# One hybrid decoder layer: gate ranks transposed a tile ahead, level copies ahead of the last doubling, one scaling moved to ScalarE

## The chip, the core and the metric

The kernel runs on one core of a Trainium2 chip. The metric is the device time in microseconds (us), the median over runs. The engines are named as in the profile: PE is TensorE (PEld its weight loads), DVE is VectorE, ACT is ScalarE, POOL is GpSimd, SP is SyncE, whose queue issues the DMA transfers. Each engine works through its own list of instructions in order; what another engine has to deliver is waited for by semaphores.

## The reference

One layer of a decoder with two groups of heads side by side, for 2048 prompt tokens and 64 sample tokens (8 sequences of 8), width 1024. Group A is attention in a window of 128 with a learned sink per head (8 query heads, 2 key heads, 64 wide), group B is gated linear attention (GLA, 4 heads, keys 64 wide, values 128 wide) whose gate has rank 16. An output projection and a squared-ReLU MLP (4096 wide) follow.

```python
# group A, softmax with a sink
m = jnp.maximum(jnp.max(scores, axis=-1, keepdims=True), sink)
p = jnp.exp(scores - m)
p = p / (jnp.sum(p, axis=-1, keepdims=True) + jnp.exp(sink - m))
# group B, log gate from the ranks, and the recurrence over chunks
log_a = jax.nn.log_sigmoid(jnp.einsum('btr,rk->btk', glr, w_gk2) + b_gk) / GLA_GATE_TEMP
S = ab[..., None] * S + jnp.einsum('bthk,bthv->bhkv', kd, vv)
o = rms_norm(o, g_gla) * jax.nn.silu(gr)
mix = jnp.einsum('bte,ed->btd', jnp.concatenate([attn, gla_out], axis=-1), w_out)
```

All matmuls are to float32's precision; the kernel splits operands into a high and a low part (fp32r), which is what names such as `ph`, `pl`, `wop` and `mt` stand for.

## The kernel before

The prompt is worked in tiles of 128 tokens (16 of them, `NB`), the sample tokens are one more tile. There are four stages, one behind the other.

**Attention (about 40 to 300 us).** The loop over tiles `i` holds four units per tile, one for each pair of query heads, (r, jj) = (0,0), (0,1), (1,0), (1,1), u = 0 to 3. The generator `unit` is one unit, cut into phases by its `yield`s: scores `sc` (PE), the mask and the maximum (DVE, into `s` and `m`), exp with the sum `den` (ACT), reciprocal and the scaling of `s` by `den` (DVE, two instructions of 128x256), transposes `pT` of `s` (PE), the copy `ph` (ACT) and the rest `pl` (DVE), the products `av` (PE), and the sum `mo` (ACT copy `rest`, then DVE). Units overlap: for each u the loop steps the units `now`, `behind` and `ahead` by their phases and puts between them the input projection's matmuls (`proj`, as many as `A_FILL` says) and other work of the tile (`A_PLAN`). The order so written holds on PE, ACT and DVE: `te`, `ac` and `dv` are `InOrder` wrappers that tie each instruction to the one before it. One step of the loop, at u, is: `next(now)`, `next(behind, None)`, `next(ahead)`, `next(now)`; the `ahead` step there is the next unit's `sc`, and the second `next(now)` is this unit's `pT`.

**GLA (about 345 to 740 us).** The generator `gla(i)` works one tile and hands back counts of filling matmuls; the main loop puts so many matmuls of the GLA projection (`gproj`) there. `G_FILL` holds the five counts. Here the order of PE follows the program, while ACT's and DVE's instructions are placed by a scheduler, within what the program's dependencies and `tc.issue_after` ties allow. What a tile does, in order:

- `qk_T`: transposes of queries and keys (`gqk`), copies `kt` (DVE) and `qz` (ACT). 34 fills follow.
- `finish_out` of the tile before: squares `ojunk` (ACT), root, `og` (DVE), transposes `ogT` (PE), copy `mo` (ACT), store.
- `decays(i + 1)` for the next tile: in even tiles of two the ranks are transposed (`pg`, PE) and copied (`glrT`, ACT), one copy for two tiles. 6 fills follow. Then the two products `z` (PE), three activations `zt` (ACT) and `before` (DVE). The second fill count stands between `pg` and `z`.
- `put_diagonal` (DVE, into AH) and the levels: for each of seven block sizes `level_sums` doubles the running sums. Per level there are two exps (ACT, `dec`, from `before` L1011 and `after` L1013) and two additions (DVE, `after` L1014 and `before` L1015), and `weighted` (DVE, `XK`, `XQ`). In the program they belong to this tile; the scheduler lets the next tile's doublings run while this tile's fills run. With the last level, `keys_decayed` makes `kdT` (ACT exp L997, DVE product) and later transposes it (PE) and copies it to `kd` (ACT L1003).
- `gate` (`sg`: ACT, DVE and two products on POOL). Then 24 fills, the `kdT` transposes, 8 fills.
- level products `gl` and `gh` (PE), the state's increment `ds` (PE, from `kd`), `qd` (DVE), the six `put_level` writes into AH (DVE, predicated copies L1021), two far copies and two near copies into AT (all ACT, L1122 and L1124; a near copy moves one half, 64x256), the two updates of the state S (DVE, L1127). 20 fills.
- `o`: four pairs of matmuls per tile, from S and `qd`, and from AT.

From tile 6 on, parts of the output weight are also split (`wop`, one 128x1024 ACT copy and one DVE subtraction each; `WO_PARTS`), tied behind `done`, the last S update. The raw part `wor` is loaded and the result `wo_d` stored by SP's queue.

PSUM is shared by `bank(shape, kind)`: a tile of a kind waits until the last one of the kind in its slot has been read. `decays(i, P, before)` uses kind "d", as do `gqk` and `ds`; `keys_decayed`, `o` and `ogT` use "e".

**Output projection and MLP (from about 740 us).** PE works them through nearly without a gap; the change leaves this code as it is.

Lines that the text below refers to: `G_FILL` L65, the scaling in `unit` L489, the loop's step L835 to L838, `decays` L933, `keys_decayed` L995, `level_sums` L1011 to L1015, `put_level` L1021, `decayed` L1060, `gla` L1067, AT L1122 and L1124, S L1127.

Of the kernel before, what the change touches and what calls it, by code (L numbers as in the profile page):

```python
# [15 lines left out]
AF = mybir.ActivationFunctionType  # L16
ALU = mybir.AluOpType
# [4 lines left out]
P = 128  # L22
# [3 lines left out]
NB = T // P  # L26
# [15 lines left out]
NL = len(LEVELS)  # L42
# [19 lines left out]
G_FIRST = (0, 1)  # L62
G_NEXT = (NB, *range(2, NB))
G_ORDER = (0, 1, 2, 3)
G_FILL = (34, 6, 24, 8, 20)  # L65
S_WAIT = (3, 6)
WO_PARTS = ((), (0, 1, 2), (3, 4, 5), (6, 7))
B_ORDER = (*(j + b for j in range(4) for b in (0, 4)), NB, *(j + b for j in range(4) for b in (8, 12)))
# [47 lines left out]
def f32(ap):  # L116
    return ap.bitcast(F32)
# [23 lines left out]
def hybrid_step_kernel(ctx: ExitStack, tc: tile.TileContext, I, O):  # L141
    nc = tc.nc
# [20 lines left out]
    te, ac, dv = (InOrder(tc, engine) for engine in (nc.tensor, nc.scalar, nc.vector))  # L163
# [4 lines left out]
    def bank(shape, kind, name):  # L168

        return ps.tile(shape, F32, tag=kind, name=name, bufs=1 if kind in "de" else 2)  # L170
# [21 lines left out]
    ident = cpool.tile([P, P], F32, name="ident")  # L192
# [77 lines left out]
    glr = gp_pool.tile([P, (NTILE + 1) // 2, 2, HD], F32R, name="glr")  # L270
# [185 lines left out]
    def unit(i, r, jj, mo):  # L456
# [29 lines left out]
        yield  # L486
        dv.reciprocal(den, den)
        for u in range(2):
            dv.tensor_scalar(s[:, u, :nk], s[:, u, :nk], den[:, u : u + 1], None, op0=ALU.mult)  # L489
        yield  # L490
        pT = bank([P, nkt, 2, P], "c", f"pT_{u_}")
        for u in range(2):
# [289 lines left out]
    for i in range(NB):  # L782
        if i + 4 < NTILE:
            load_x(i + 4)
        if i == NB - 1:
            wa_pool.release()
            w_pools.append(open_gw(G_LATE))
            for n in range(4):
                stage = ("w_raw", 2) if n % 2 else ("x", 2)
                weights.append((*load_gw(*late.popleft(), *stage), stage))  # L790
        elif i >= 3:
            for _ in range(min(2, len(early))):
                weights.append((*load_gw(*early.popleft()), None))
        store()
        if i == 4:
            wgk, msk, smsk, dmsk, onehot, ggla = load_consts()
        if i == NB - 4:
            nc.sync.dma_start(smask, I["c_smask"])
            cached.update({(name, 0): load_cache(name, 0) for name in "kv"})
        if i >= NB - 2:  # L800
            t = i - NB + 2
            gxTs[t] = load_T(t, [sp.tile([P, KT, P], F32R, tag=x, name=f"g{x}_{t}", bufs=2) for x in ("xh", "xl")])
            fill = chain(fill, projecting(t, gxTs[t], G_EARLY, ac))
        new = i + 3 < NTILE
        todo["turn"] = lambda: run(rotate(i + 1))
        if i + 2 < NTILE:
            todo["first"] = lambda: take_first(i + 2)
            todo["rest"] = lambda: todo.update(vl=take_rest(i + 2))
        if new:
            todo["junk"] = lambda: todo.update(rstd=x_norm(i + 3))  # L810

        def do(u, phase):
            for name, at in A_PLAN:
                if at == (u, phase) and name in todo:
                    todo.pop(name)()

        for u in range(4):
            for unit_ in (behind, now) if u in A_PL_FIRST else (now, behind):
                next(unit_, None)
            next(now)  # L820
            do(u, "A")
            later = next(queue)
            next(later)
            run(fill, A_FILL[u][0])
            next(behind, None)
            next(behind, None)
            run(fill, A_FILL[u][1])
            if u < 2 and new:
                hi, todo[f"x{u}"] = x_half(i + 3, u)
                hi()  # L830
            elif u == 2:
                todo.update(heads_T(i + 1))
            do(u, "X")
            run(fill, A_FILL[u][2])
            next(now)  # L835
            next(behind, None)
            next(ahead)
            next(now)  # L838
            do(u, "B")
            split_some(A_SPLIT[u] if i < NB - 1 else 1)  # L840
            next(now)
            do(u, "C")
            behind, now, ahead = now, ahead, later
# [86 lines left out]
    for t in (s_xk, s_qz, s_at, s_after):  # L930
        nc.gpsimd.memset(t, 0.0)

    def decays(i, n, before, kind="d"):  # L933

        gt = glrT[i // 2 % 2 if i < NB else 2]
        if i % 2 == 0:
            pg = bank([P, P], kind, f"pg_{i}")
            te.transpose(pg, f32(glr[:, i // 2]).rearrange("p a r -> p (a r)"), ident)
            nc.scalar.activation(gt, pg, AF.Copy)
        yield  # L940
        z = bank([P, 2, n], kind, f"z_{i}")
        for g in range(2):
            te.matmul(z[:, g], wgk[:, i % 2, g * P : (g + 1) * P], gt[:, :n], start=True, stop=True)
        t = next(zts)[:, :, :n]
        nc.scalar.activation(t, z, AF.Abs)
        nc.scalar.activation(t, t, AF.Exp, scale=-1.0)
        nc.scalar.activation(t, t, AF.Ln, bias=1.0)
        nc.vector.scalar_tensor_tensor(before, z, 0.0, t, op0=ALU.min, op1=ALU.subtract)
# [43 lines left out]
        out = xq[:, l].rearrange("p r g (m b) -> p r (g m) b", b=b)  # L992
        nc.vector.tensor_tensor(out, dr.unsqueeze(1).to_broadcast(list(out.shape)), pairs(q, b, 1), op=ALU.mult)

    def keys_decayed(after, kt, kdT, n, kind, kd):  # L995

        nc.scalar.activation(kdT, after, AF.Exp, scale=1.0 / 16)  # L997
        nc.vector.tensor_tensor(kdT, kdT, kt, op=ALU.mult)
        yield
        pk = bank([P, 2, P], kind, f"kdT_{n}")  # L1000
        for g in range(2):
            te.transpose(pk[:n, g, :], kdT[:, g, :], ident)
        nc.scalar.activation(kd[:n], pk[:n].rearrange("p g k -> p (g k)"), AF.Copy)  # L1003

    def level_sums(before, after, dec, l, b):

# [53 lines left out]
    def decayed(i):  # L1060

        before, after = next(befores), next(afters)
        yield from decays(i, P, before)
        nc.gpsimd.memset(after, 0.0)
        pre[i] = before, after

    def gla(i, gp, og=iter(())):  # L1067
# [8 lines left out]
        following = decayed(i + 1) if i < NB - 1 else iter(())  # L1076
        yield G_FILL[0] if i else 24, True
        deque(og, 0)
        next(following, None)
        yield G_FILL[1], True  # L1080
        put_diagonal(i, AH, gp, P)
        for l, b in enumerate(LEVELS):
            level_sums(before, after, dec, l, b)
            if l == NL - 1:
                kd = next(kds)
                turned = keys_decayed(after, kt, next(kdTs), P, "e", kd)
                nc.scalar.activation(dec[:, NL], before, AF.Exp, scale=1.0 / 16)
            weighted(XK, XQ, dec, kt, qz, l, b)
        next(turned)
        deque(following, 0)  # L1090
        assert {(i, c) for c in range(4)} <= projected
        sg = gate(i, gp, P)
        yield G_FILL[2], True
# [26 lines left out]
            put_level(AH, gm, msk[:, l], LEVELS[l])  # L1120
        for g in range(2):
            nc.scalar.activation(AT[:HD, 2 * g : 2 * g + 2, HD:], far[half_of[g]], AF.Copy)  # L1122
        for uu in half_of:
            nc.scalar.activation(AT[uu, :, uu], AH[uu], AF.Copy)  # L1124
        So, Sn = S[i % 2], S[(i + 1) % 2]
        for g in range(2):
            done = nc.vector.scalar_tensor_tensor(  # L1127
                Sn[:, g], So[:, g], dec[:, NL, g, P - 1 : P], ds[:, g], op0=ALU.mult, op1=ALU.add
            )
        yield G_FILL[4], True  # L1130
        o_ = bank([P, 4, P], "e", f"o_{i}")
        for h in range(4):
# [204 lines left out]
        vector.tensor_tensor(x[:n], x1[:n], x[:n], op=ALU.add)  # L1337
        nc.sync.dma_start(x1_d[i], x[:n])

    wo, pre, ogs_of, mixes, late_mix = {}, {}, {}, {}, []  # L1340
    wo_parts = iter(())
    early = []
    fill = products()
# [758 lines left out]
```

## Time and profile before

| | |
|---|---|
| median of 3 runs | 2243.93 us (2241.8 to 2244.42) |
| the profiled execution | 2241.18 us, of which the span of its trace 2239.4 us |
| granted TensorE clock, mean | 0.996 of full speed |
| PE busy | 2173.6 us of the span (97%) |
| DVE, ACT, POOL busy | 1531.7, 1217.7, 261.3 us |

A row of the timeline gives start, duration, engine, line, operation and output<-inputs with the shape of one and the number of instructions (x); a stretch of a few equal neighbours is one row, whose duration runs from the first's start to the last's end. In square brackets stands how long the engine was idle just before, and what ended it. In the list of waits a row gives the engine and what it ran next, what it waited for, and then us in total, number of times and the longest. In rows of groups the figures after the bar are busy time and the mean of one in ns, then the idle time before. The lines that most helper calls go through are one (L130), so groups are told apart by the tiles' names.

### The profile page before, as it was taken

Reading aid. Unit: us, or ns where it says so; the run is one execution under the profiler, and the core shown is the slowest. Engines: PE = TensorE matmul, PEld = TensorE weight load, DVE = VectorE, ACT = ScalarE, POOL = GpSimd, SP = SyncE. Lnnn points to the kernel's source line nnn. Section 1 sums busy time; section 2 is a strip of 40 time slices with the busy share of each in tenths; the row PEclk is TensorE's granted clock in tenths of the full one; section 3 lists DMA queues with packets and bytes.
Section 4 is the critical chain, followed back from the end, with each engine's and each line's share of the span. In section 5 each row is a group of like instructions: output and inputs, shape, how many; then the busy total and the mean of one; then the engine's idle time right before and its main releaser. Section 6 shows DMA issues by size and latency. Waiting matters only on the chain.

```text
span 2239.4 us, 34249 instructions
## 1 busy us (share of the span) xinstructions
PE 2173.6 (97%) x11784; PEld 1865.2 (83%) x11784; DVE 1531.7 (68%) x3117; ACT 1217.7 (54%) x2610; POOL 261.3 (12%) x417
## 2 busy tenths in 40 slices
PE   8999999999999999899999999999999999999998
PEld 7888888999998788788888788888788888888886
DVE  5888876766775566788888755447776666555566
ACT  5777766656665344455555554335444444544444
POOL 3566422112111100000000000000000000000000
PEclk9999999999999999999999999999999999999999
DMA  7334332224345559877777787657654444766684
GB/s 233 120 129 139 100 103 64 67 76 144 109 142 193 177 175 315 299 240 252 266 258 249 265 279 242 186 182 234 204 185 155 155 151 150 263 199 196 195 257 150
DMA packets 242314, 419.92 MB, mean 188 GB/s; under 512 B 26132, under 2 KB 142332, under 8 KB 238028
## 3 DMA queue, kind: packets, MB, share of 16 engines
q1 hardware_dynamic: 242140, 417.74, 56.3%
q8 instruction: 93, 1.52, 0.3%
q14 instruction: 81, 0.66, 0.1%
HBM read 270.53 MB, written 148.18 MB: 187 GB/s over the span
## 4 chain that ended last, share of the span: by engine, by line
PE 73%; DVE 13%; ACT 7%; DMA 4%; issue 2%; POOL 1%; SPq 0%; DVEq 0%; ACTq 0%; POOLq 0%
PE dn L130 26%; PE ua L130 7%; PE uc L130 7%; PE gproj L130 6%; PE out L1250 6%; PE ud L130 4%; PE ue L130 4%; PE ub L130 4%; DVE s L130 2%; PE proj L130 2%; PE dsam L130 1%; PE sam L130 1%; DVE pl L130 1%; PE o L130 1%; DMA rt<-t_d 1%
## 5 line engine op out<-in xcount | busy, mean ns | idle before, releaser
L130 PE MATMUL dn<-o0t,o0s 128*128 128x512 f32 x896 | 349.9, 391 | 2.5 <-DVE samq L130 2.0
L130 PE MATMUL dn<-o1t,o0s 128*128 128x512 f32 x896 | 350.7, 391 | 0.9 <-DVE o1t L219 0.7
L130 PE MATMUL dn<-o0t,o1s 128*128 128x512 f32 x896 | 350.0, 391 | 0.0
L219 DVE TENSOR_TENSOR o1s<-rs,o0s 128x512 fp32r<-128x512 f32 x224 | 154.7, 691 | 234.0 <-ACT o0s L218 230.4
L218 ACT ACTIVATE o0s<-rs 128x512 fp32r<-128x512 f32 x224 | 141.1, 631 | 298.9 <-PE dn L130 280.2
L130 PE MATMUL gproj<-wg,gx 128*128 128x384 f32 x1408 | 268.5, 343 | 0.0
L130 PEld LDWEIGHTS gproj<-wg,gx 128*128 128x128 f32 x1408 | 241.6, 190 | 4.2 <-issue 3.9
L130 ACT ACTIVATE st<-st 128x512 f32<-128x512 f32 x224 | 141.2, 630 | 137.7 <-DVE st L130 133.6
L130 PEld LDWEIGHTS dn<-o0t,o0s 128*128 128x128 f32 x896 | 168.6, 188 | 39.8 <-issue 2.4
L130 PEld LDWEIGHTS dn<-o1t,o0s 128*128 128x128 f32 x896 | 168.6, 188 | 38.5 <-DVE o1t L219 2.8
L130 PEld LDWEIGHTS dn<-o0t,o1s 128*128 128x128 f32 x896 | 168.7, 188 | 35.1
L130 PE MATMUL uc<-H,s 128*128 128x512 f32 x768 | 186.4, 391 | 0.0
L130 PE MATMUL ua<-H,w 128*128 128x512 f32 x744 | 179.2, 390 | 0.0
L130 PEld LDWEIGHTS uc<-H,s 128*128 128x128 f32 x768 | 143.1, 188 | 30.3
L130 PEld LDWEIGHTS ua<-H,w 128*128 128x128 f32 x744 | 139.7, 188 | 29.4
L1250 PE MATMUL out<-wo,mt 128*128 128x512 f32 x680 | 158.9, 392 | 1.7 <-ACT mt L218 1.7
L219 DVE TENSOR_TENSOR o1t<-rt,o0t 128x512 fp32r<-128x512 f32 x224 | 153.4, 685 | 8.2 <-ACT o0t L218 8.0
L208 POOL TENSOR_TENSOR frs<-rs_v,half 128x1 f32<-128x1 f32 (+1 forms) x13 | 10.0, 779 | 1211.1 <-DVE rs_v L206 691.1
L1250 PEld LDWEIGHTS out<-wo,mt 128*128 128x128 f32 x680 | 126.5, 188 | 28.4 <-ACT mt L218 1.9
L218 ACT ACTIVATE o0t<-rt 128x512 fp32r<-128x512 f32 x224 | 138.5, 618 | 16.5 <-DMA rt<-t_d 10.4
L130 DVE TENSOR_TENSOR st<-st 128x512 f32<-128x512 f32 x160 | 110.7, 692 | 27.2 <-ACT st L130 23.0
L130 ACT ACTIVATE s<-t 128x1024 fp32r<-128x1024 f32 x62 | 65.8, 1061 | 97.0 <-PE ua L130 27.9
(388 smaller groups left out, 4231.1 us busy)
## 6 DMA issues: line engine op xcount, KB each, us to landing
s_d<-st SPq DMA_DIRECT2D x32, 1792.0 KB, 8.7
rs<-s_d SPq DMA_DIRECT2D x224, 256.0 KB, 3.5
raw<-in_w_up SPq DMA_DIRECT2D x64, 512.0 KB, 4.7
rt<-t_d SPq DMA_DIRECT2D x128, 256.0 KB, 4.0
rt<-in_w_down SPq DMA_DIRECT2D x96, 256.0 KB, 3.1
t<-in_w_down SPq DMA_DIRECT2D x64, 256.0 KB, 3.9
t_d<-t SPq DMA_DIRECT2D x32, 512.0 KB, 3.3
gx<-xt_d SPq DMA_DIRECT2D x28, 512.0 KB, 5.4
```

The costliest lines, as they stand in the source:

```text
L130: ins = call(*a, **k)
L208: nc.gpsimd.tensor_tensor(out, v[:n], e, op=ALU.pow)
L218: nc.scalar.activation(hi, src, AF.Copy)
L219: vector.tensor_tensor(lo, src, f32(hi), op=ALU.subtract)
L1250: te.matmul(banks[c], x, w[:, c * 512 : (c + 1) * 512], start=k + u == 0, stop=k == KT - 1 and u == len(products) - 1,)
```

## The change

1. `G_FILL` becomes (34, 14, 16, 8, 20): the same sum. The second count moves behind the levels and behind `z`, so in a tile `z` follows `ogT` at once, and then come 14 + 16 fills.
2. The ranks of tiles 2k and 2k + 1 are transposed in the third slot of `keys_decayed`'s bank, one tile ahead (in even tile i for the pair i/2 + 1), and copied to `glrT` right after `kd`. Only tile 0 and the sample tile keep their own `pg`. In tile 0 `decays` uses kind "b".
3. Of the two near copies into AT, DVE makes one (`put[0]`) and ACT the other. The last level's sums of a tile beyond the first, and both S updates, are tied behind `put[0]` on the engine's list.
4. `done` is now ACT's near copy, so the `wop` splits are tied behind that, and not behind S.
5. In attention the scaling of unit (1,1) goes to ACT as two activations with `den` as the scale. At u = 3 the loop steps `now` (this `pT`) first, then `behind` and `ahead` (`sc`).

By the lists of instructions DVE has 32 scalings fewer and 16 copies into AT more; ACT the other way about. PE's list has the same instructions in another order. On ACT the order around the AT copies in tile 9 was `kdT`, `gp`, D (the exp of `before` for all of the tile), two far copies, two near copies, squares `ojunk`, with `wop` behind the squares of the tile; it is now two far copies, one near copy, `wop`, `kdT`, D, squares. On DVE the last doubling and S now stand between the copy into AT and the next tile's `kt`, with the diagonal write behind S and ahead of the doubling.

```diff
--- before.py
+++ after.py
@@ -62,7 +62,7 @@
 G_FIRST = (0, 1)
 G_NEXT = (NB, *range(2, NB))
 G_ORDER = (0, 1, 2, 3)
-G_FILL = (34, 6, 24, 8, 20)
+G_FILL = (34, 14, 16, 8, 20)
 S_WAIT = (3, 6)
 WO_PARTS = ((), (0, 1, 2), (3, 4, 5), (6, 7))
 B_ORDER = (*(j + b for j in range(4) for b in (0, 4)), NB, *(j + b for j in range(4) for b in (8, 12)))
@@ -486,7 +486,10 @@
         yield
         dv.reciprocal(den, den)
         for u in range(2):
-            dv.tensor_scalar(s[:, u, :nk], s[:, u, :nk], den[:, u : u + 1], None, op0=ALU.mult)
+            if (r, jj) == (1, 1):
+                ac.activation(s[:, u, :nk], s[:, u, :nk], AF.Copy, scale=den[:, u : u + 1])
+            else:
+                dv.tensor_scalar(s[:, u, :nk], s[:, u, :nk], den[:, u : u + 1], None, op0=ALU.mult)
         yield
         pT = bank([P, nkt, 2, P], "c", f"pT_{u_}")
         for u in range(2):
@@ -833,9 +836,14 @@
             do(u, "X")
             run(fill, A_FILL[u][2])
             next(now)
-            next(behind, None)
-            next(ahead)
-            next(now)
+            if u == 3:
+                next(now)
+                next(behind, None)
+                next(ahead)
+            else:
+                next(behind, None)
+                next(ahead)
+                next(now)
             do(u, "B")
             split_some(A_SPLIT[u] if i < NB - 1 else 1)
             next(now)
@@ -930,14 +938,17 @@
     for t in (s_xk, s_qz, s_at, s_after):
         nc.gpsimd.memset(t, 0.0)
 
+    def ranks_T(pair, out):
+        te.transpose(out, f32(glr[:, pair]).rearrange("p a r -> p (a r)"), ident)
+        return out
+
     def decays(i, n, before, kind="d"):
 
         gt = glrT[i // 2 % 2 if i < NB else 2]
-        if i % 2 == 0:
+        if i in (0, NB):
             pg = bank([P, P], kind, f"pg_{i}")
-            te.transpose(pg, f32(glr[:, i // 2]).rearrange("p a r -> p (a r)"), ident)
-            nc.scalar.activation(gt, pg, AF.Copy)
-        yield
+            nc.scalar.activation(gt, ranks_T(i // 2, pg), AF.Copy)
+            yield
         z = bank([P, 2, n], kind, f"z_{i}")
         for g in range(2):
             te.matmul(z[:, g], wgk[:, i % 2, g * P : (g + 1) * P], gt[:, :n], start=True, stop=True)
@@ -992,15 +1003,18 @@
         out = xq[:, l].rearrange("p r g (m b) -> p r (g m) b", b=b)
         nc.vector.tensor_tensor(out, dr.unsqueeze(1).to_broadcast(list(out.shape)), pairs(q, b, 1), op=ALU.mult)
 
-    def keys_decayed(after, kt, kdT, n, kind, kd):
+    def keys_decayed(after, kt, kdT, n, kind, kd, pair=0):
 
         nc.scalar.activation(kdT, after, AF.Exp, scale=1.0 / 16)
         nc.vector.tensor_tensor(kdT, kdT, kt, op=ALU.mult)
         yield
-        pk = bank([P, 2, P], kind, f"kdT_{n}")
+        pk = bank([P, 3, P], kind, f"kdT_{n}")
         for g in range(2):
             te.transpose(pk[:n, g, :], kdT[:, g, :], ident)
-        nc.scalar.activation(kd[:n], pk[:n].rearrange("p g k -> p (g k)"), AF.Copy)
+        ranks = ranks_T(pair, pk[:, 2]) if pair else None
+        nc.scalar.activation(kd[:n], pk[:n, :2].rearrange("p g k -> p (g k)"), AF.Copy)
+        if pair:
+            nc.scalar.activation(glrT[pair % 2], ranks, AF.Copy)
 
     def level_sums(before, after, dec, l, b):
 
@@ -1060,7 +1074,7 @@
     def decayed(i):
 
         before, after = next(befores), next(afters)
-        yield from decays(i, P, before)
+        yield from decays(i, P, before, "d" if i else "b")
         nc.gpsimd.memset(after, 0.0)
         pre[i] = before, after
 
@@ -1076,18 +1090,22 @@
         following = decayed(i + 1) if i < NB - 1 else iter(())
         yield G_FILL[0] if i else 24, True
         deque(og, 0)
-        next(following, None)
-        yield G_FILL[1], True
         put_diagonal(i, AH, gp, P)
         for l, b in enumerate(LEVELS):
-            level_sums(before, after, dec, l, b)
+            if l < NL - 1 or i == 0:
+                level_sums(before, after, dec, l, b)
+            else:
+                with tc.issue_after(put[0].ins):
+                    level_sums(before, after, dec, l, b)
             if l == NL - 1:
                 kd = next(kds)
-                turned = keys_decayed(after, kt, next(kdTs), P, "e", kd)
+                pair = i // 2 + 1 if i % 2 == 0 and i < NB - 2 else 0
+                turned = keys_decayed(after, kt, next(kdTs), P, "e", kd, pair)
                 nc.scalar.activation(dec[:, NL], before, AF.Exp, scale=1.0 / 16)
             weighted(XK, XQ, dec, kt, qz, l, b)
         next(turned)
         deque(following, 0)
+        yield G_FILL[1], True
         assert {(i, c) for c in range(4)} <= projected
         sg = gate(i, gp, P)
         yield G_FILL[2], True
@@ -1120,13 +1138,14 @@
             put_level(AH, gm, msk[:, l], LEVELS[l])
         for g in range(2):
             nc.scalar.activation(AT[:HD, 2 * g : 2 * g + 2, HD:], far[half_of[g]], AF.Copy)
-        for uu in half_of:
-            nc.scalar.activation(AT[uu, :, uu], AH[uu], AF.Copy)
+        put[:] = [nc.vector.tensor_copy(AT[half_of[1], :, half_of[1]], AH[half_of[1]])]
+        done = nc.scalar.activation(AT[half_of[0], :, half_of[0]], AH[half_of[0]], AF.Copy)
         So, Sn = S[i % 2], S[(i + 1) % 2]
-        for g in range(2):
-            done = nc.vector.scalar_tensor_tensor(
-                Sn[:, g], So[:, g], dec[:, NL, g, P - 1 : P], ds[:, g], op0=ALU.mult, op1=ALU.add
-            )
+        with tc.issue_after(put[0].ins):
+            for g in range(2):
+                nc.vector.scalar_tensor_tensor(
+                    Sn[:, g], So[:, g], dec[:, NL, g, P - 1 : P], ds[:, g], op0=ALU.mult, op1=ALU.add
+                )
         yield G_FILL[4], True
         o_ = bank([P, 4, P], "e", f"o_{i}")
         for h in range(4):
@@ -1337,7 +1356,7 @@
         vector.tensor_tensor(x[:n], x1[:n], x[:n], op=ALU.add)
         nc.sync.dma_start(x1_d[i], x[:n])
 
-    wo, pre, ogs_of, mixes, late_mix = {}, {}, {}, {}, []
+    wo, pre, ogs_of, mixes, late_mix, put = {}, {}, {}, {}, [], []
     wo_parts = iter(())
     early = []
     fill = products()
```

## The prediction

> **What bounds the kernel now.** I began with the page's first section and the stretches of the span, because TensorE (PE) is busy nearly throughout.
>
> ```profile
> span 2239.4 us, 34249 instructions
> PE 2173.6 (97%) x11784; PEld 1865.2 (83%) x11784; DVE 1531.7 (68%) x3117; ACT 1217.7 (54%) x2610; POOL 261.3 (12%) x417
> ...
> core 0: us, PE busy (x) PEld busy (x) DVE busy (x) ACT busy (x) POOL busy (x), PEclk, DMA share, GB/s
> 40.00:300.00 260.00, 244.55 (x1604) 224.19 (x1603) 223.68 (x663) 198.42 (x549) 145.88 (x264) 1.00 0.37 125
> 345.00:740.00 395.00, 375.59 (x3045) 353.72 (x3044) 274.28 (x840) 248.40 (x722) 69.27 (x74) 1.00 0.36 117
> ```
>
> PE stands idle 2239.4 − 2173.6 = 65.8 us. The change leaves the PE's matmuls as they are (only their order moves), so all it can save is idle PE time in the two stages that it edits: attention (40 to 300), 260 − 244.55 = 15.5 us, and gated linear attention, GLA (345 to 740), 395 − 375.59 = 19.4 us. So I read next what PE waits for up to 760 us (columns: total, times, longest).
>
> ```profile
> PE o L130 <- ACT AT L1124: 10.8, 9, 2.2
> PE pT L130 <- DVE s L130: 8.2, 21, 0.5
> ...
> PE gqk L130 <- DVE before L948: 3.3, 1, 3.3
> PE z L130 <- ACT glrT L939: 3.0, 4, 0.9
> ```
>
> The four waits named by the change sum to 10.8 + 8.2 + 3.3 + 3.0 = 25.3 us. That is the most it can win directly, and each needs its own reason.
>
> **Level copies and what is ahead of them (GLA).** Tile 9 shows the o wait, first on VectorE (DVE), then on ScalarE (ACT), then on PE.
>
> ```profile
> 589.49 0.29 DVE L1014 TENSOR_TENSOR after<-after,before 128x128 f32<-128x128 f32 x1
> 590.09 1.58 DVE L1021 COPY_PREDICATED AH<-c,gl 128x128 f32<-128x128 uint8 x4
> 592.03 0.34 DVE L1127 SCALAR_TENSOR_TENSOR S<-S,dec,ds 128x128 f32<-128x128 f32 x1
> ...
> 592.73 0.54 ACT L1122 ACTIVATE AT<-gh 64x128 f32<-64x128 f32 x2
> 593.17 0.83 ACT L1124 ACTIVATE AT<-AH 64x256 f32<-64x256 f32 x2
> ...
> 594.05 0.49 PE L130 MATMUL o<-gp,AT 128*128 128x128 f32 x2 [1.56 <-ACT AT L1124]
> 596.07 6.14 PE L130 MATMUL gproj<-wg,gx 128*128 128x384 f32 x34
> 602.05 0.60 PE L130 MATMUL ogT<-ident,og 128*128 128x128 f32 x4
> ```
>
> The last doubling (it starts at 589.49; the AH writes at 590.09) stands ahead of the AH writes, the two S updates (the second at 592.03) stand between those, and ACT copies both AT halves one after the other. After the change the six AH writes follow the doubling before the last; then DVE copies one half and ACT the other, side by side, and S and the last doubling come behind. Taken away ahead of o: 590.09 − 589.49 = .6 for the doubling; at most 2 x .34 for S, of which I take .5 since neighbours overlap a little; half of the .83 us on ACT, .4; and ACT's far copies (.54) can now run beside DVE's copy, worth up to .5. In all 1.5 to 2.0 us a tile. The first eight waits are 10.8 − 2.16 = 8.6 us together, 1.1 each, and the longest is tile 8's; they go. Only the ninth, tile 14's 2.16, stays in part:
>
> ```profile
> 570.54 0.49 PE L130 MATMUL o<-gp,AT 128*128 128x128 f32 x2 [1.72 <-ACT AT L1124]
> ...
> 703.97 1.22 DVE L219 TENSOR_TENSOR mt<-mt 128x1024 fp32r<-128x1024 f32 x1
> 709.02 0.49 PE L130 MATMUL o<-gp,AT 128*128 128x128 f32 x2 [2.16 <-ACT AT L1124]
> ```
>
> Its AH writes come behind a split of mt (1.22, the second of two), which the change leaves where it is, and now behind its diagonal sums too; I leave 1.3 us of 2.16. Gain: 10.8 − 1.3 = **9.5 us**. Bounds: 10.8 when all goes; 6 when only S and ACT's half count (.9 a tile, 8 x .9 = 7.2 at most, less in the waits shorter than .9, nothing in tile 14).
>
> What is late next? The moved work: A6, B6, then kdT of the same tile and kd, all behind the AT copy. The weight split wop (ACT) is moved too: it was tied to the S updates and ran among ACT's later work; now it comes right behind ACT's AT copy, with kdT and D (the exps of `after` and `before`, 128x256 each), all ahead of the squares (ojunk) that o's normalisation needs.
>
> ```profile
> L218 ACT ACTIVATE wop<-wor 128x1024 fp32r<-128x1024 f32 x8 | 8.5, 1057 | 0.8 <-DMA wor<-in_w_out 0.8
> ...
> 589.81 0.42 ACT L997 ACTIVATE kdT<-after 128x256 f32<-128x256 f32 x1
> 595.92 0.28 ACT L1037 ACTIVATE ojunk<-o 128x128 bf16<-128x128 f32 x1 [1.92 <-PE o L130]
> 600.29 0.64 ACT L954 ACTIVATE sg<-gp 128x512 f32<-128x512 f32 x1 [0.49 <-DVE og L1042]
> ```
>
> 1.06 + 2 x .42 = 1.9 us, while PE's o lasts from 594.05 to about 595.9, 1.9 us as well. So ojunk starts about when it would. Even if late it has slack: ACT saw og finished at 600.29, and ogT runs at 602.05, behind the 34 fill matmuls: about 1.8 us. Cost 0; without that cover, each us of lateness past 1.8 costs PE one us, in the eight tiles with wop first. SP's order changes with it: the loads of wor move a few places against the stores of wo_d. The eight wor loads waited .8 us in all, so I take 0.
>
> kd is now copied one or two exps later on ACT, and ds needs it:
>
> ```profile
> 586.69 0.31 ACT L1011 ACTIVATE dec<-before 128x128 f32<-128x128 f32 x1
> 586.91 0.36 ACT L1003 ACTIVATE kd<-kdT 128x256 f32<-128x256 f32 x1
> 587.99 0.61 PE L130 MATMUL ds<-gp,kd 128*64 128x128 f32 x8
> ```
>
> kd was done at 587.27, .7 us ahead of ds; two exps of .31 use that up. I charge **−1.0 us** in all (0 to −4: .3 us in each of 13 tiles).
>
> **Ranks a tile ahead.** In even tiles PE transposes the ranks (pg) and six fills later wants z, while ACT's glrT copy waits its turn in the queue. The change transposes with kdT one tile earlier; the copy comes behind kd. The same nine copies remain, and the fills are only divided anew (6 + 24 = 14 + 16). All four z waits vanish: **3.0 us** (bounds 2.5 to 3.0). z comes 6 fills (6 x 6.14/34 = 1.1 us) earlier, but its next steps are behind ACT's gate chain, so I count nothing for that.
>
> Tile 0's gqk no longer waits for `before`, since the ranks' and z's tile now sits in another bank:
>
> ```profile
> 355.10 0.42 DVE L948 SCALAR_TENSOR_TENSOR before<-z,zt 128x256 f32<-128x256 f32 x1 [1.50 <-ACT zt L947]
> 355.58 0.66 PE L130 MATMUL gqk<-ident,gp 128*128 128x128 f32 x4 [3.34 <-DVE before L948]
> ```
>
> But tile 0's doublings need the same `before`. PE goes on to its 24 fills (24 x .18 = 4.3 us) and meets kdT and AT, which start no earlier than 355.5. Most of the 3.34 comes back there. I take **.6 us** (bounds 0 and 3.3 + .8, the latter with tile 1's ogT wait).
>
> **Scale by ACT in attention.** The last unit of each tile, on the three engines:
>
> ```profile
> 229.23 1.51 DVE L130 TENSOR_SCALAR s<-s,den 128x256 f32<-128x256 f32 x2
> ...
> 228.85 1.74 POOL L386 TENSOR_TENSOR tb<-qk,rope 128x320 f32<-128x320 f32 x2
> ...
> 229.57 0.59 ACT L130 ACTIVATE ql<-pq 64x512 fp32r<-64x512 f32 x1
> ...
> 229.58 0.28 PE L130 MATMUL sc<-kl,qh 128*128 128x256 f32 x1
> 230.02 0.41 PE L130 MATMUL pT<-ident,s 128*128 128x128 f32 x2 [0.16 <-DVE s L130]
> 230.89 0.41 PE L130 MATMUL pT<-ident,s 128*128 128x128 f32 x2 [0.47 <-DVE s L130]
> 231.05 0.43 PE L130 MATMUL proj<-wa_hi,xl 128*128 128x392 f32 x1
> 234.39 0.76 DVE L130 TENSOR_SCALAR s<-s,den 128x256 f32<-128x256 f32 x2
> ```
>
> Two scales here take 1.51 us beside POOL's tb; two alone take .76 (234.39).
>
> [...]
>
> ACT has no row of this shape. Nearest from below: zt 128x256 at .42 (L946). From above: the 128x384 scaling of wg at .61.
>
> ```profile
> L946 ACT ACTIVATE zt<-zt 128x256 f32<-128x256 f32 x16 | 6.7, 417 | 0.4
> L130 ACT ACTIVATE wg<-wg_raw,gcol 128x384 fp32r<-128x384 f32 x16 | 8.8, 607 | 0.0
> ```
>
> I take .45, near the row of the same size. ACT is free for them at 229.57, where ql starts now, so the pairs of pT go at 230.05 and 230.5 in place of 230.02 and 230.89. But the change also puts pT ahead of the sc matmuls (the last starts at 229.58): they no longer cover the wait but follow it, some .5 us. Then proj starts at about 230.5 + .2 + .5 = 231.2 against 231.05: .1 to .2 lost, and ql and the ph copy stand .9 later on ACT. Against it, DVE is 1.51 us freer for mo and the next reduce, which PE waits for later in the tile. I take **0** for the stage: between −6 (.61 a scale: +.36 a tile x 16) and +4 (.25 a tile).
>
> [...]
>
> **The sum.** −9.5 − 3.0 − .6 + 1.0 + 0 = −12.1 us. The profiled execution took 2241.18 us (its span of 2239.4 and 1.8 around it), so 2229.1. The median of the three runs, 2243.93, lies 2.75 above it; on that footing **2232 us**.
>
> **The rivals.**
> 1. More is won, 2222 us: the whole of tile 0's wait and tile 1's ogT wait (3.3 + .8 − .6 = 3.5), attention's upper bound (4), the rest of o (1.3) and no kd wait (1.0): 9.8 more. For it: attention's pT waits are 8.2 us. Against: its work is unchanged in amount, and only sits on another engine.
> 2. Nothing measurable, 2241 us: what is freed at o is given back at the next waits, 3 us more in ds (4 in place of 1) and .36 x 16 = 5.8 in attention's uncovered pT: −12.1 + 3 + 5.8 = −3.3. For it: in attention the sc cover is really taken off. Against: kd's margin of .7 us, and a scale price nearer .42 than .61.
> 3. Slower, 2251 us: ACT's new queue between AT and ojunk holds the ring. From the point where ojunk starts more than 1.8 us after o's end, each us is PE's at ogT. In series with waits between them (kdT needs A6, which stands behind AT, S and S on DVE; wop needs its wor load), wop, kdT and D could put ojunk 3.8 us late in the eight tiles with wop and 2.4 late in six others: 8 x 2.0 + 6 x .6 = 19.6, and −12.1 + 19.6 = +7.5. For it: tile 1, where ogT did wait for og:
>
> ```profile
> 383.05 0.66 PE L130 MATMUL ogT<-ident,og 128*128 128x128 f32 x4 [0.82 <-DVE og L1042]
> ```
>
>    Against: 1.9 us of new work beside 1.9 us of o, and wor loads that have been waited for .8 us in all.
>
> **How the numbers follow.** Forecast 2232: .56; rival 1: .12; rival 2: .17; rival 3: .15. A measurement of this kernel can tell .2% (4.5 us) from no change; so faster .56 + .12 and little of rival 2, .69; same .16; slower .15. The forecast's own range, from the bounds of o (6 to 10.8), kd (0 to −4), tile 0 (0 to 4) and attention (−6 to +4) taken not all at once, is 2225 to 2239. The range reaches over most of rival 1 and rival 2: 2221 to 2244.
>
> **What would show it.** Right: the list of PE's waits has o <- AT near 1 us and no z <- glrT; in tile 9 a DVE copy of AT beside ACT's, S after it; PE idle in 345 to 740 falls from 19.4 to about 8; that in 40 to 300 stays near 15.5. Wrong in the level copies: o waits still over 4 us. Wrong in the cover: ogT <- og, or ds <- kd, above 4 us. Wrong in attention: its idle above 18 or below 12, with the ACT scale far from .45. Wrong altogether: a wait in the MLP or for wo that was not there.

## The result and the profile after

| | before | changed |
|---|---|---|
| median (5 runs each) | 2241.81 us | 2231.76 us |
| lowest to highest | 2241.59 to 2244.42 | 2227.12 to 2234.79 |
| the profiled execution, its span | 2241.18, 2239.4 us | 2234.79, 2233.0 us |
| ratio, 95% interval | | 0.9949, 0.9933 to 0.9965 |

The changed kernel is faster by about .5%. The profiled execution is the slowest of its five, so its span shows less of the gain than the median; its clock is told under the hardware.

The page and the stretches of the changed kernel:

```profile
span 2233.0 us, 34187 instructions
PE 2174.4 (97%) x11784; PEld 1868.1 (84%) x11784; DVE 1521.8 (68%) x3101; ACT 1219.5 (55%) x2626; POOL 261.0 (12%) x417
...
40.00:300.00 260.00, 242.12 (x1606) 225.38 (x1606) 203.96 (x634) 210.35 (x580) 145.79 (x264) 0.99 0.37 125
345.00:740.00 395.00, 387.41 (x3104) 364.22 (x3104) 288.46 (x867) 240.35 (x712) 71.11 (x76) 0.99 0.37 122
```

PE's idle time in the GLA stretch fell from 19.4 to 395 − 387.41 = 7.6 us; the forecast said about 8. In the attention stretch it rose from 15.5 to 17.9. What PE waited for up to 760 us says why:

```profile
PE pT L130 <- ACT s L130: 15.4, 16, 1.4
...
PE o L130 <- DVE S L1146: 2.2, 2, 1.6
PE gproj L130 <- ACT dec L1025: 1.8, 1, 1.8
...
PE o L130 <- ACT AT L1142: 1.3, 1, 1.3
...
PE gproj L130 <- DVE gp_s L213: 0.9, 1, 0.9
```

The z waits and tile 0's gqk wait are not in this list any more, and the o waits are 2.2 + 1.3 = 3.5 us in place of 10.8. The pT waits nearly doubled, from 8.2.

Tile 9 of the changed kernel, on DVE, then ACT, then PE:

```profile
585.76 1.57 DVE L1035 COPY_PREDICATED AH<-c,gl 128x128 f32<-128x128 uint8 x4
587.44 0.64 DVE L1035 COPY_PREDICATED AH<-c,gh 128x128 f32<-128x128 uint8 x2
588.11 0.29 DVE L1141 COPY AT<-AH 64x256 f32<-64x256 f32 x1
588.43 0.61 DVE L1146 SCALAR_TENSOR_TENSOR S<-S,dec,ds 128x128 f32<-128x128 f32 x2
...
589.35 0.28 DVE L1028 TENSOR_TENSOR after<-after,before 128x128 f32<-128x128 f32 x1
...
588.11 0.56 ACT L1140 ACTIVATE AT<-gh 64x128 f32<-64x128 f32 x2 [1.20 <-DVE AH L1035]
588.57 0.40 ACT L1142 ACTIVATE AT<-AH 64x256 f32<-64x256 f32 x1
588.88 1.05 ACT L218 ACTIVATE wop<-wor 128x1024 fp32r<-128x1024 f32 x1
589.82 0.40 ACT L1008 ACTIVATE kdT<-after 128x256 f32<-128x256 f32 x1
...
591.23 0.28 ACT L1051 ACTIVATE ojunk<-o 128x128 bf16<-128x128 f32 x1 [0.70 <-PE o L130]
...
589.25 0.38 PE L130 MATMUL o<-S,qd 128*128 128x128 f32 x2
...
597.37 0.60 PE L130 MATMUL ogT<-ident,og 128*128 128x128 f32 x4
```

From the first AH write to the end of AT are now 588.97 − 585.76 = 3.2 us; before the change it was 594.00 − 590.09 = 3.9, and the last doubling came ahead of that. AT is ready .3 us before PE reaches o, so there is no wait. wop, kdT and the other exp fit between AT and the end of o: ACT even stood idle .70 us until o was done, and ogT comes with no wait.

Where the 6.4 us between the two spans lie can be read from two landmarks of PE: pT, attention's transposes, and ds, GLA's state products. The rows give number of instructions, shortest, median and longest in ns, and first and last start; the first two are of the kernel before, the last two of the changed one:

```profile
L130 PE MATMUL pT<-ident,s x248: 270/273/304, 42.5 to 315.4; 128*128 128x128 f32 x124
L130 PE MATMUL ds<-gp,kd x128: 272/273/324, 370.6 to 732.0; 128*64 128x128 f32 x128
...
L130 PE MATMUL pT<-ident,s x248: 270/273/332, 42.5 to 315.9; 128*128 128x128 f32 x124
L130 PE MATMUL ds<-gp,kd x128: 272/273/323, 373.5 to 723.1; 128*64 128x128 f32 x128
```

Attention (first to last pT): 272.9 before, 273.4 after. From there to the first ds: 55.2 and 57.6, 2.4 lost. GLA (first to last ds): 361.4 and 349.6, 11.8 won. From the last ds to the end: 1507.4 and 1509.9, 2.5 lost in code that the change leaves alone. Each of the four stretches of the changed trace holds one spell of half clock more than before, 1.7 us each; these spells are told under the hardware. Without them attention would have won an estimated 1.2 us in place of losing .5, GLA 13.5, and the losses of 2.4 and 2.5 would be .7 and .8.

### The profile page after: what moved, and what is told of

The parts are those of the page before. It is cut to its first block, busy times and chain, and to the rows that moved or that the text cites. A ratio compares the mean times of both kernels' runs of the same rounds, so it can differ in the third digit from the quotient of the medians.

```text
span 2233.0 us, 34187 instructions
## 1 busy us (share of the span) xinstructions
PE 2174.4 (97%) x11784; PEld 1868.1 (84%) x11784; DVE 1521.8 (68%) x3101; ACT 1219.5 (55%) x2626; POOL 261.0 (12%) x417
## 4 chain that ended last, share of the span: by engine, by line
PE 77%; ACT 7%; DVE 7%; DMA 5%; issue 2%; POOL 0%; SPq 0%; DVEq 0%; ACTq 0%; POOLq 0%
PE dn L130 24%; PE gproj L130 9%; PE uc L130 7%; PE ua L130 7%; PE out L1269 6%; PE ub L130 4%; PE ud L130 4%; PE ue L130 4%; PE proj L130 2%; ACT s L130 2%; PE sam L130 1%; PE dsam L130 1%; PE o L130 1%; DMA rt<-t_d 1%; DVE s L130 1%
```

## The experiments

Each was run against the kernel before on the same chip; the ratios are to that (the changed kernel: 0.9949). Names: the changed kernel is C. Times of C were taken in another group of runs, so small differences between an experiment and C are read from the traces.

**The GLA part alone.** C with the attention part undone.

```diff
-            if (r, jj) == (1, 1):
-                ac.activation(s[:, u, :nk], s[:, u, :nk], AF.Copy, scale=den[:, u : u + 1])
-            else:
-                dv.tensor_scalar(s[:, u, :nk], s[:, u, :nk], den[:, u : u + 1], None, op0=ALU.mult)
+            dv.tensor_scalar(s[:, u, :nk], s[:, u, :nk], den[:, u : u + 1], None, op0=ALU.mult)
...
-            if u == 3:
-                next(now)
-                next(behind, None)
-                next(ahead)
-            else:
-                next(behind, None)
-                next(ahead)
-                next(now)
+            next(behind, None)
+            next(ahead)
+            next(now)
```

> Attention as before (scaling on VectorE, old order at u = 3), all of the change's GLA part kept. Theory (the whole gain is GLA's, attention costs a little because pT now waits uncovered): about 2.5 us faster than the changed kernel, 13 to 14 us faster than before. Rival (attention is neutral, and the 2.9 us by which the changed trace reaches the first GLA tile later is its lower clock): equal to the changed kernel within 1 us, about 11 us faster than before.

2231.47 us, ratio 0.9946 (0.9933 to 0.9959). The rival was right: by time it is equal to C, and its trace takes 55.2 us from the last pT to the first ds, as before the change, where C has a spell of half clock more.

**The attention part alone**, put into the kernel before.

> The kernel before with the attention part alone (scaling of the last unit on ScalarE, pT ahead of sc). Theory: 2 to 3 us slower than before, PE's pT waits go from 8.2 to about 15 us. Rival (neutral): within 1 us of before. A second rival (ScalarE's scaling pays by itself): 3 to 5 us faster.

2241.85 us, ratio 0.9995 (0.9987 to 1.0004): neutral, as the first rival had it, though PE's pT waits are 15.6 us, as the theory had it. The two runs together settle that the whole gain of C that the times can show is GLA's.

**The scaling on ScalarE, with the old order at u = 3.**

```diff
-            if u == 3:
-                next(now)
-                next(behind, None)
-                next(ahead)
-            else:
-                next(behind, None)
-                next(ahead)
-                next(now)
+            next(behind, None)
+            next(ahead)
+            next(now)
```

> The changed kernel with the scaling on ScalarE but the old order at u = 3 (sc ahead of pT). Theory (it is the lost cover of four sc, about .47 us a tile, that costs): 5 to 7 us faster than the changed kernel, pT waits near 8 us again. Rival (pT later makes ph and av later, PE waits there instead): within 2 us of the changed kernel, with new av waits.

2217.84 us (2215.46 to 2218.93), ratio 0.9889 (0.9876 to 0.9901): 25 us under before, about 14 under C, twice what the theory gave. It is the fastest kernel of the study. Some 3.5 us of the 14 are an estimate of what its higher clock gave (on average .9958 granted in its runs, .9942 in C's: .0016 x 2232). Its landmarks:

```profile
L130 PE MATMUL pT<-ident,s x248: 270/272/331, 41.5 to 304.6; 128*128 128x128 f32 x124
L130 PE MATMUL ds<-gp,kd x128: 272/273/323, 358.3 to 706.8; 128*64 128x128 f32 x128
```

Attention takes 263.1 us, 10.3 less than in C, of which 1.7 are a spell of half clock in C's trace at 54 us; from there to the first ds it is 53.7, 3.9 less, where C's trace has two spells (3.4) and this one none. GLA, 348.5, is as in C (349.6). The place on PE, C first, then this kernel:

```profile
228.92 0.34 PE L130 MATMUL proj<-wa_lo,xh 128*128 128x392 f32 x1
230.21 0.84 PE L130 MATMUL pT<-ident,s 128*128 128x128 f32 x4 [0.95 <-ACT s L130]
230.81 0.36 PE L130 MATMUL sc<-kh,qh 128*128 128x256 f32 x1
...
231.36 0.34 PE L130 MATMUL proj<-wa_hi,xl 128*128 128x392 f32 x1
...
220.60 0.34 PE L130 MATMUL proj<-wa_lo,xh 128*128 128x392 f32 x1
221.04 0.36 PE L130 MATMUL sc<-kh,qh 128*128 128x256 f32 x1
...
221.90 0.84 PE L130 MATMUL pT<-ident,s 128*128 128x128 f32 x4
222.49 0.42 PE L130 MATMUL proj<-wa_hi,xl 128*128 128x392 f32 x1
```

From the last proj ahead to the first proj behind, C takes 231.36 − 228.92 = 2.44 us, this kernel 222.49 − 220.60 = 1.89. In C PE stands .95 us before pT and only then does sc; here sc runs in that time. The same difference of starts, as a mean over twelve tiles of each trace: before 2.35, C 2.46, this kernel 1.91. The step after it, u = 0 with xT, also shrinks: 1.78 before, 1.59 in C, 1.47 here. So ScalarE's scaling wins .44 + .31 us a tile, and the order gives .55 + .12 of it back. From one tile's xT to the next one's, a whole tile of the kind read here takes 17.49 us before, 17.40 in C and 16.75 in this kernel.

**The new order with the scaling on VectorE.**

> The changed kernel with the scaling back on VectorE but the new order at u = 3 (pT ahead of sc). Theory: VectorE's pair takes 1.5 us beside POOL and starts .4 us earlier than ScalarE's, which takes .9; so pT comes about .2 us later per tile: 2 to 4 us slower than the changed kernel. Rival (the order alone matters): within 1 us of it.

2236.12 us, ratio 0.9964 (0.9952 to 0.9977), 4.4 us above C by the medians, a little more than the theory gave, and 3.4 by the ratios, within it; the intervals of the two overlap. The traces are clearer: the stretch at u = 3 takes 2.90 us by the same mean, .44 more than in C and .55 more than before the change. With either engine the new order costs .55 us there. What it costs over a whole tile differs: with VectorE the step at u = 0 gets .25 shorter (1.53 against 1.78), and a tile takes 17.73 us, .24 more than before; with ScalarE it is .65 (17.40 against 16.75).

**Without the two ties on VectorE** (the last doubling and S may go ahead of the AH writes).

```diff
-                with tc.issue_after(put[0].ins):
-                    level_sums(before, after, dec, l, b)
+                level_sums(before, after, dec, l, b)
...
-        with tc.issue_after(put[0].ins):
-            for g in range(2):
+        for g in range(2):
```

> The changed kernel without the two ties on VectorE: the last doubling and the state updates may stand ahead of the AH writes again; the copy split between VectorE and ScalarE stays. Theory (the order on VectorE is over half of the gain, about 1.1 of 2.0 us a tile): the o waits come back in part, 3 to 5 us in tiles 5 to 12, time 3 to 5 us above the changed kernel. Rival (the copy split alone is enough): within 1 us, o waits as in the changed kernel.

2236.45 us, ratio 0.9967 (0.9955 to 0.9979), 4.7 us above C.

**Without the split of the copy** (both near copies on ScalarE, the ties kept, behind the last AH write).

```diff
+        put[:] = [last]
...
-        put[:] = [nc.vector.tensor_copy(AT[half_of[1], :, half_of[1]], AH[half_of[1]])]
+        nc.scalar.activation(AT[half_of[1], :, half_of[1]], AH[half_of[1]], AF.Copy)
```

> The changed kernel with both near copies of AT on ScalarE again, last doubling and S still tied behind the last AH write. Theory (the split is worth about .9 us a tile, the order the rest): o waits near 3 us in all against 3.5 in the changed kernel's tiles 1, 5 and 14 plus under .3 elsewhere, time 1 to 3 us above the changed kernel. Rival (the split is what removes the waits): 6 to 8 us above it.

2233.37 us, ratio 0.9955 (0.9943 to 0.9967). The lists of waits of these two up to 760 us:

```profile
PE o L130 <- ACT AT L1138: 7.8, 10, 1.7
...
PE o L130 <- ACT AT L1143: 6.1, 5, 2.1
```

Against 3.5 us in C, the ties are worth 4.3 us of o waits and the split 2.6. Neither alone removes them. For the ties the theory was right (4.0 us of waits in tiles 5 to 12); for the split the waits came out at twice the 3 us that the theory gave, and the time (1.6 us above C, within the intervals) as it said. So the ties are shown by time and waits, the split by its waits alone.

**Ranks back in their own tile**, fills 6 + 24, tile 0 in bank d.

```diff
-G_FILL = (34, 14, 16, 8, 20)
+G_FILL = (34, 6, 24, 8, 20)
...
-        if i in (0, NB):
+        if i % 2 == 0:
...
-                pair = i // 2 + 1 if i % 2 == 0 and i < NB - 2 else 0
+                pair = 0
```

> The changed kernel with the ranks transposed in their own tile again, the fills 6 + 24, and tile 0's gate products in bank d. Theory: the four z waits (3.0 us) and the gqk wait (3.3 us, of which .6 net) are back: 3 to 4.5 us above the changed kernel. Rival (tile 0's wait was the larger part): 5 to 7 us above. Rival (z's waits only covered others): within 1 us.

2233.9 us, ratio 0.9958 (0.9946 to 0.9969). By time alone this isn't clear of C; the waits are:

```profile
PE gqk L130 <- DVE before L959: 3.2, 1, 3.2
PE z L130 <- ACT glrT L950: 2.9, 4, 0.8
```

Both are back as they were, 6.1 us in all, and the time is 2.1 us above C, under the 3 to 4.5 forecast. Part of the difference is the clock: this kernel's runs were granted .9960 on average, C's .9942, and .0018 x 2232 is an estimated 4 us in favour of this kernel.

**wop behind S again.** `done`, the tie of wop, is set once more by the last S update.

```diff
-                nc.vector.scalar_tensor_tensor(
+                done = nc.vector.scalar_tensor_tensor(
```

> The changed kernel with the wop splits tied behind the last S update, as before the change, in place of ScalarE's copy. Theory (wop between AT and the squares is covered): within 1.5 us of the changed kernel, no ogT waits in either. Rival (wop delays squares, og and ogT): 2 to 4 us faster than the changed kernel.

2232.07 us, ratio 0.995 (0.9938 to 0.9962): as C, and no ogT wait in either. wop between AT and the squares is covered.

**POOL behind VectorE's scaling.** To see whether POOL's tb makes VectorE's scaling slow, POOL first copies one column of the scaled s. The scheduler left tb ahead of that copy, so this first try tells nothing of it.

```diff
+        if (r, jj) == (1, 1):
+            nc.gpsimd.tensor_copy(late_turn, s[:, 1, :1])
```

> GLA part of the change, attention with the scaling on VectorE and the old order (as e1), but POOL copies one element column of the scaled s before it goes on, so that POOL's tb begins behind the scaling. Theory (VectorE's scaling is slow only because POOL's tb runs beside it): the pair takes .76 in place of 1.5 us, pT waits fall from 8 to under 3 us, time 8 to 14 us below e1, near e3. Rival (something else makes it slow, or tb a microsecond later is waited for): within 2 us of e1.

2230.53 us, ratio 0.9938 (0.9926 to 0.9951), the pair still 1.51 us. The second try ties tb behind it:

```diff
+            with tc.issue_after(held[0].ins) if held else ExitStack():
...
+            held[:] = [nc.gpsimd.tensor_copy(late_turn, s[:, 1, :1])]
```

> As e12, with POOL's tb tied behind its one-column copy of the scaled s, since in e12 tb still ran ahead of that copy (228.72 against 232.05). Theory (VectorE's scaling is slow only because POOL's tb runs beside it): the pair takes .76 in place of 1.51 us, PE's pT waits in attention fall from 8 to under 3 us, and the time falls 6 to 12 us below e1, near e3's 2218. Rival (its slowness has another cause): the pair stays at 1.5 us, and the time is within 2 us of e1. Second rival (VectorE's next work meets tb instead, kl, mo or the reduce): pair .76, but less than half of the time gained.

2225.27 us, ratio 0.9928 (0.9915 to 0.9942). The scaling of the last unit and of the next one on DVE, and POOL behind the first and beside the second:

```profile
228.55 0.62 DVE L130 TENSOR_SCALAR s<-s,den 128x256 f32<-128x256 f32 x2
...
232.81 1.64 DVE L130 TENSOR_SCALAR s<-s,den 128x256 f32<-128x256 f32 x2
...
229.46 1.71 POOL L389 TENSOR_TENSOR tb<-qk,rope 128x320 f32<-128x320 f32 x2
231.25 1.56 POOL L395 TENSOR_TENSOR qk<-qk,rope 128x640 f32<-128x640 f32 x1
...
232.90 1.40 POOL L398 TENSOR_TENSOR rot<-qk,tb 128x512 f32<-128x512 f32 x1
```

With POOL out of its way the pair takes .62 us in place of 1.51: the cause is shown. But POOL's work, moved back by .7 us, now stands beside the next unit's scaling (rot, from 232.90), which takes 1.64 in place of .76. The second rival had foreseen a collision further on, with other work of VectorE. By the mean over twelve tiles the stretch at u = 3 falls from 2.35 to 1.47 and that at u = 0 rises from 1.78 to 2.59: nothing is won in the stage (a tile takes 17.49 us, as before). Its pT waits are 8.5 us, as in the kernel with the GLA part alone; that this run is faster than that one (4 us by the ratios) lies outside attention, and part of it in fewer spells of half clock; it isn't settled further.

**The scaling ahead of rest**, on the fastest kernel.

```diff
             next(behind, None)
+            if u == 3:
+                next(now)
             next(behind, None)
             run(fill, A_FILL[u][1])
...
+            if u < 3:
+                next(now)
```

> e3 (ScalarE's scaling, old order) with the scaling at u = 3 ahead of the copy rest on ScalarE. Theory (pT in e3 still waits about .3 us a tile because ScalarE makes rest first): 2 to 4 us below e3. Rival (mo comes .9 us later and the unit's next steps wait for it): 0 to 3 us above e3.

2225.75 us, ratio 0.9916 (0.9902 to 0.9929): 6 us slower by the ratios (.0027 x 2242). The stretch at u = 3 falls to 1.69, but rest and mo come later, and the next steps wait, longer than either forecast had it (a tile takes 17.41 us, .66 more):

```profile
PE av L130 <- DVE pl L130: 3.3, 13, 0.3
PE av L130 <- DVE rs_v L130: 2.2, 11, 0.3
```

**The old order in the last tile only**, on C.

```diff
-            if u == 3:
+            if u == 3 and i < NB - 1:
```

> The changed kernel, but in the last of the 16 tiles the old order at u = 3. Theory (two waits close together at 315 us set off a spell of half clock, 3.4 us long, that costs 1.7 us beside the waits): the spell at 316 to 320 is gone, PE reaches the GLA stage 2.5 to 3.5 us earlier. Rival (the clock falls there anyway): .5 us earlier, spell still there.

2228.53 us, ratio 0.9925 (0.9911 to 0.9938).

```profile
L130 PE MATMUL ds<-gp,kd x128: 272/273/323, 369.5 to 718.7; 128*64 128x128 f32 x128
```

The first ds comes 4.0 us earlier than in C (369.5 against 373.5), .5 more than the theory gave, and the rows of the granted clock under the hardware below show the spell gone. But the theory isn't shown by that. Of the 4.0 us, .6 lie ahead of the first pT (41.9 against 42.5), and the other 3.4 are two spells that C's trace has and this one has not, the one at 316 us and another at 368. And four experiments with C's order in the last tile have its two waits and no spell at 316 either. By time the run is not clear of C: the intervals overlap.

## Why the prediction was right, point by point

- **The total.** 2232 us was forecast, 2231.76 measured; the forecast's −12.1 stands beside −10.05 by the medians and −11.4 by the ratio (0.0051 x 2241.81). Faster, as forecast. That the time was met to .2 us is luck: the forecast started from 2243.93, the median before was 2241.81 this time, and the gain came out 2 us short.
- **GLA's sum.** It is right by misses that cancel: the o waits gave 2.2 less than forecast, while ds gave 1.4 more (.4 won in place of 1.0 lost) and tile 1's ogT .8 more. PE's idle time fell by 11.8 us.
- **Level copies, −9.5.** Right in kind, too large by 2.2: the o waits fell from 10.8 to 3.5 (7.3). Tile 14 kept 1.55 where I left 1.3, and tiles 1 and 5 kept .6 and 1.3 where I left nothing. I had taken all eight shorter waits to be queues of the last doubling and S. In tile 5 the AH writes stand behind the sample tile's output, which waits for POOL, and the change does not touch that:

```profile
498.32 1.13 DVE L1056 SCALAR_TENSOR_TENSOR gp_s<-s_ob,ors,s_sg 64x128 f32<-64x128 f32 x4 [1.11 <-POOL ors L208]
499.37 1.57 DVE L1035 COPY_PREDICATED AH<-c,gl 128x128 f32<-128x128 uint8 x4
```

- **z, −3.0.** Right: the four waits are gone, and come back when the ranks do.
- **Tile 0, −.6.** Right to the tenth: 3.34 at gqk became .92 + 1.82 ahead of kdT. That most would come back there was argued; the tenth is luck, since no row gave the share.
- **kd, +1.0.** Too high: no wait of ds is left in the list, where .4 us was before. The exps now ahead of kd used at most its margin.
- **wop and the squares, 0.** Right. The ring that rival 3 feared had .70 us to spare in tile 9.
- **Attention, 0.** Right as a sum, and the largest thing that I missed inside it. I had .1 to .2 us a tile lost at the scaling and something won on DVE behind it, and so it was: .11 lost at u = 3 (2.46 against 2.35), .19 won at u = 0 (1.59 against 1.78). In truth ScalarE's scaling alone is worth some .75 us a tile and the new order takes .67 of it back. The step that hid it was pricing the change as one block: I counted the lost cover of sc at some .5 us, correctly, but against an unchanged order I never asked what the scaling alone would bring, where ACT's .90 (the pair in the changed kernel; I had taken .45 each) replaces 1.51 under the same cover. Three readings there were not exact. The .76 of a pair "alone" stood beside short copies of POOL. ACT did have a nearer row, attention's exp of 128x257 at .50, against .497 measured for each scaling. And at .61 a scale a tile loses 2 x .16 = .32 us, not .36, which would make the bound −5 and rival 2's time 2240; the forecast does not use it.
- **Rivals 1 and 2** held in pieces that cancel: tile 1's ogT wait (.8) did go, the pT waits grew by 7.2.

The same edit is neutral in one order and wins in the other, since VectorE's pair costs 1.51 us beside POOL against ScalarE's .90. Beside an idle POOL VectorE's pair took .62, less than ScalarE's.

## What to carry to other kernels

Price the engine an operation is moved to and the order in which it is issued separately: the move alone was worth 10 us in its stage here, and together they were worth nothing. Before work is taken off an engine that another one slows, look at what will stand beside that other one next: here the collision moved with it (.62 us in place of 1.51 at one scaling, 1.64 in place of .76 at the next). A wait list gives the sum of a kind of wait, but each one has its own queue ahead, and the largest error in the forecast's terms came from treating eight alike. Before a difference of a few us is put down to a change, set the granted clocks beside each other: here .001 of it is an estimated 2.2 us (.001 x 2232).

## What the runs showed of the hardware

**Spells of half clock.** In 2 us slices through the span, the granted clock (the last column but two) falls to about .50 for 3.4 us at a time, once in the changed kernel for 6.8 (from 932 us). Two waits of PE close together, .75 and .69 us, are followed by such a spell in the changed kernel. With the old order in the last tile, whose waits there are .32 and .18, it stays at 1.00, but also in the kernel without the two ties, which has the same waits as the changed one. The rows are of these three, the changed kernel first, then the old order in the last tile, then without the ties:

```profile
315.38 0.84 PE L130 MATMUL pT<-ident,s 128*128 128x128 f32 x4 [0.75 <-ACT s L130]
317.35 0.45 PE L130 MATMUL ssc<-kc,qs 64*32 64x128 f32 x8 [0.69 <-ACT kc L130]
316.00:318.00 2.00, 1.31 (x23) 0.91 (x21) 0.17 (x1) 1.30 (x3) 0.00 (x0) 0.92 0.06 19
318.00:320.00 2.00, 2.00 (x6) 2.00 (x7) 1.53 (x5) 0.68 (x3) 0.00 (x0) 0.50 0.62 168
320.00:322.00 2.00, 2.00 (x11) 2.00 (x11) 0.64 (x3) 0.45 (x3) 0.21 (x1) 0.72 0.12 43
...
318.00:320.00 2.00, 2.00 (x14) 2.00 (x14) 1.09 (x7) 1.33 (x5) 0.53 (x1) 1.00 0.35 98
...
315.78 0.84 PE L130 MATMUL pT<-ident,s 128*128 128x128 f32 x4 [0.75 <-ACT s L130]
317.74 0.45 PE L130 MATMUL ssc<-kc,qs 64*32 64x128 f32 x8 [0.69 <-ACT kc L130]
318.00:320.00 2.00, 2.00 (x26) 1.91 (x17) 1.71 (x5) 0.68 (x2) 0.00 (x0) 1.00 0.50 141
```

Such a spell costs 2 x (.08 + .50 + .28) = 1.7 us, more than either wait. Of the six traces with these two waits, the changed kernel and the one with the attention part alone have the spell, the four without the ties, without the split, with the ranks back and with wop behind S have not. The wait of 1.82 us in tile 0 is followed by one in the changed kernel (.50 at 370) and by none in the fastest kernel, which has 1.83 us there. So the same waits may or may not be followed by a spell, and whether they set it off isn't shown.

From 30 us on, up to the last 12, the profiled execution before has four spells (6.8 us), that of the changed kernel as much as eight (13.7 us; the one of 6.8 us counts as two). The difference, 6.8, is an estimate of what the clock hid of the gain between the two spans: 6.4 + 6.8 = 13.2 us at the same clock. The spread of the runs goes with the clock as well. In the changed kernel's five runs, from slowest to fastest, the mean granted clock is .993, .993, .994, .995 and .996; .003 x 2232 is 6.7 of the 7.7 us between them. Which executions get more spells, and why, wasn't tried.

Past the first 40 us no wait of PE is longer than 3.34 us in the kernel before (tile 0's gqk) and 2.96 us in the changed one (up to 932.69 us). How long a wait has to be for a spell to follow, or whether a spell needs one, these runs don't show.

**VectorE beside POOL.** A pair of 128x256 scalings took .62 us with POOL idle (at 224.46 us before the change, and at 228.55 with POOL's tb tied behind), .76 and .94 beside POOL's short copies kl (at 234.39 before and 234.34 in the changed kernel), 1.51 beside its tensor-tensor work tb (at 229.23 before) and 1.64 beside rot (at 232.81 with tb tied). With POOL's work moved, the slow pair moved: .62 in place of 1.51 at the last unit, 1.64 in place of .76 at the next one.
